# One level of Strassen's scheme in the up-projection of an MLP: seven half-width products instead of eight, with GpSimd forming the weight sums

## The chip, the cores and the metric

The kernel runs on one core of a Trainium2 chip. The time is device microseconds of one launch, the median of several executions. The engines are TensorE (PE in the profile, its weight loads PEld), VectorE (DVE), ScalarE (ACT), GpSimd (POOL) and SyncE (SP, which here issues the weight loads).

## The reference, cut to what matters

Two layers act on 512 tokens of width 1024, in float32. Each layer has three attention branches, whose gated sum goes through `w_out`, and then the MLP:

```python
x = x + merged @ w_out[l]
u = rmsnorm(x, g_mlp[l]) @ w_mlp1[l]                 # (512 x 1024) @ (1024 x 4096)
x = x + jnp.square(jax.nn.relu(u)) @ w_mlp2[l]       # (512 x 4096) @ (4096 x 1024)
```

## The kernel before, in words

Activations lie transposed: a tile is 128 features by 512 tokens. Every float32 matrix product is made of three passes in a rounded float32 format: an operand is split into a high part `hi` and a rest `lo`, and `mm3` adds hi x hi, hi x lo and lo x hi into one PSUM bank. A weight unit is 128 x 1024 floats (512 KB). It is loaded by SP into a raw buffer `wraw`, then ACT copies it, rounded, to `whi`, and DVE subtracts `whi` from `wraw` into `wlo`; this pair of instructions is called a split below. There are `RB` = 3 raw buffers and `NB` = 4 pairs of `whi` and `wlo`.

The program is a list of entries, each with the weight units it consumes. The loop at the end goes through it; ahead of each entry it emits splits up to `NB` units in front and loads up to `RB` units in front of those. A scheduler then orders the instructions of each engine and gives out buffers from free pools; within an engine instructions run strictly in the order that it wrote.

The end of a layer, which the change touches, is this sequence:

- eight `out_item`s: output projection, residual sum into the tile `X`, and `feed`, which makes the hi and lo tiles `h2` of the MLP's input (in pool `O`) and adds the squares up in `sq2`; after the last one `row_stats` turns the squares into the factors 1/rms of the tokens: PE sums over the features (`tok_sums`, line 236), DVE makes `ms`, POOL raises it to the power -1/2 (`r`), PE broadcasts `r` to all partitions (line 247), ACT copies this to `R`;
- `u_item`s, 32 a layer: 24 matmuls of 512 columns, DVE applies ReLU and `R2`, ACT squares twice, DVE makes the rest;
- `w2_item`s, 32 a layer: 24 matmuls of 512 columns on the up-projection's result, DVE adds them to `X`. They come in four stretches of eight, d(0) to d(3), one for each quarter `qr` of the 4096 features, in the order u0 u1 d0 u2 d1 u3 d2 d3.

In `chunk256`, which the change leaves alone, attention's projections use matmuls of 256 columns.

Of the kernel before, what the change touches and what calls it, by code (L numbers as in the profile page):

```python
# [9 lines left out]
F32 = mybir.dt.float32  # L10
# [49 lines left out]
def tile_trunk(ctx: ExitStack, tc: tile.TileContext, x_t, mem_t, mem_n, pos, ifr, gcol, grow, w_ck, w_cq, w_kvb, w_qb,  # L60
# [47 lines left out]
    def mm3(o, l, r, first, last):  # L108
        T.matmul(o, lhsT=l[0], rhs=r[0], start=first, stop=False)  # L109
        T.matmul(o, lhsT=l[0], rhs=r[1], start=False, stop=False)  # L110
        T.matmul(o, lhsT=l[1], rhs=r[0], start=False, stop=last)  # L111
# [28 lines left out]
    def trig():  # L140
# [44 lines left out]
        G.dma_start(out=lvt.rearrange("p (l d) -> p l d", l=L), in_=grow[:, 128:384].partition_broadcast(P))  # L185
# [93 lines left out]
    def layer(l):  # L279
# [13 lines left out]
        def begin():  # L293
            if l == 0:
# [464 lines left out]
        def y8_item(ft):  # L759
            def fn(w):  # L760
# [4 lines left out]
                hi, lo = tl("H", F32R), tl("H", F32R)  # L765
# [7 lines left out]
        def out_item(ft):  # L773
            def fn(w):
# [9 lines left out]
                if ft == KT - 1:  # L784
                    _, _, s["R2"] = row_stats(s["sq2"])
            return Entry(fn, [w_out[l, ft]])

        def u_item(qr, j):
            def fn(w):
                q = ps("s")  # L790
                for k in range(KT):
                    mm3(q, (w[0][0][:, k, :], w[0][1][:, k, :]), s["h2"][k], k == 0, k == KT - 1)
                z = tl("scr")
                V.scalar_tensor_tensor(out=z, in0=q, scalar=0.0, in1=s["R2"], op0=ALU.max, op1=ALU.mult)
                hi, lo = (tl("H" if qr % 2 == 0 else "B", F32R) for _ in range(2))
                A.activation(out=hi, in_=z, func=AF.Square)
                A.activation(out=z, in_=z, func=AF.Square)
                V.tensor_tensor(out=lo, in0=z, in1=hi, op=ALU.subtract)
                s.setdefault(("u", qr), []).append((hi, lo))
            return Entry(fn, [w_1[l, qr * 8 + j]])  # L800

        def w2_item(qr, ft):
            def fn(w):
                q = ps("acc")
                for k in range(KT):
                    mm3(q, (w[0][0][:, k, :], w[0][1][:, k, :]), s["u", qr][k], k == 0, k == KT - 1)
# [9 lines left out]
                st["h"].append(feed(l + 1, ft, xt, C_MIX, "H", st["sqs"]))  # L816
# [48 lines left out]
    units = [ap for e in prog for ap in e.units]  # L865
    raws, splits = [], []
    consumed = 0

    def load_raw():
        ap = units[len(raws)]  # L870
        a, b = ap.shape[1], ap.shape[2]
        t = pw_raw.tile([P, 1024], F32, tag="wraw", name=nm("wraw"))
        nc.sync.dma_start(out=t[:, :a * b].rearrange("p (a b) -> p a b", a=a), in_=ap)
        raws.append((t, a, b))
# [102 lines left out]
```

## Time and profile before

| what | us |
|---|---|
| median of 3 runs | 2050.37 (2050.34 to 2050.54) |
| span of the profiled execution, first to last instruction | 2047.5 |
| what lies around the span, by the median | 2.9 |
| PE busy | 2025.8 |
| DVE busy | 1125.5 |
| ACT busy | 870.5 |
| POOL busy | 152.4 |

The profiled execution's own time is not given beside its span; its span and the median differ by 2.9 us, and the sums are made with that. The profile is a page and the answers that the trace of the same execution gives: groups of instructions by line, engine and shape, with busy time and the mean of one; waits by who waited for whom; timelines; and stretches with each engine's busy time. The time at a row's start in a timeline is in us from the span's start. A busy PE counts overlapping matmuls once, so its busy time is not matmul work; the distance from start to start is.

### The profile page before, as it was taken

The numbers are of one execution on the slowest core, as the hardware profiler recorded it, in microseconds if no ns is written. First come the engines' busy times: TensorE is split into PE (matmuls) and PEld (weight loads), VectorE is DVE, ScalarE is ACT, GpSimd is POOL, SyncE is SP. The second block draws the span as 40 slices with busy tenths as digits, with TensorE's granted clock in tenths as the row PEclk, the third lists the DMA queues.
The fourth block names the chain that finished last, engine by engine and source line by source line (L and its number), as shares of the span: only waits on it lengthen the run. The fifth ranks groups of instructions, "written<-read, shape, count | busy, mean of one in ns | idle before, by whom it ended". The sixth has DMA issues, their size and how long they took to land.

```text
span 2047.5 us, 28283 instructions
## 1 busy us (share of the span) xinstructions
PE 2025.8 (99%) x11280; PEld 1735.7 (85%) x11280; DVE 1125.5 (55%) x2058; ACT 870.5 (43%) x1607; POOL 152.4 (7%) x125
## 2 busy tenths in 40 slices
PE   8999999999999999999999999999999999999999
PEld 7889997888878888888888999978897788888887
DVE  7754665667656443443457546657685554434442
ACT  6565543444443442322345645444454334323221
POOL 2300110101100000000003001101020000000000
PEclk9999999999999999999999999999999999999999
DMA  5242122222214333333333321212222233333332
GB/s 178 78 140 74 63 65 60 73 73 63 73 48 150 96 97 94 102 93 101 118 95 94 115 72 63 67 58 73 73 63 63 92 124 93 94 102 93 101 94 73
DMA packets 54036, 181.09 MB, mean 88 GB/s; under 512 B 6176, under 2 KB 6704, under 8 KB 53904
## 3 DMA queue, kind: packets, MB, share of 16 engines
q1 hardware_dynamic: 51840, 175.66, 28.0%
q10 hardware_dynamic: 1872, 3.21, 0.5%
q8 instruction: 89, 1.46, 0.3%
q0 software_dynamic: 192, 0.41, 0.1%
q14 instruction: 43, 0.35, 0.1%
HBM read 175.06 MB, written 4.19 MB: 88 GB/s over the span
## 4 chain that ended last, share of the span: by engine, by line
PE 97%; ACT 1%; DMA 1%; DVE 1%; issue 0%; SPq 0%; POOL 0%; POOLq 0%; ACTq 0%
PE psacc L109 21%; PE psacc L110 20%; PE psacc L111 20%; PE pss L109 7%; PE pss L110 7%; PE pss L111 7%; PE pso L642 4%; PE pss L609 3%; PE pss L612 2%; PE pstp L638 2%; PE pstp L649 1%; PE pstp L590 1%; PE pstp L478 1%; DMA X<-in_x_t_dram 0%; DMA B<-in_mem_n_dram 0%; PE pstp L236 0%
## 5 line engine op out<-in xcount | busy, mean ns | idle before, releaser
L101 ACT ACTIVATE whi<-wraw 128x1024 fp32r<-128x1024 f32 (+3 forms) x320 | 334.5, 1047 | 726.8 <-PE psacc L110 354.5
L102 DVE TENSOR_TENSOR wlo<-wraw,whi 128x1024 fp32r<-128x1024 f32 (+3 forms) x320 | 386.0, 1207 | 103.1 <-ACT whi L101 101.8
L109 PE MATMUL psacc<-H,whi 128*128 128x512 f32 x816 | 322.0, 395 | 1.3 <-ACT B L560 1.3
L110 PE MATMUL psacc<-H,whi 128*128 128x512 f32 x816 | 321.1, 393 | 0.0
L111 PE MATMUL psacc<-H,wlo 128*128 128x512 f32 x816 | 319.6, 392 | 0.0
L109 PE MATMUL psacc<-whi,H 128*128 128x256 f32 (+1 forms) x928 | 272.8, 295 | 7.2 <-ACT whi L101 5.8
L110 PE MATMUL psacc<-wlo,H 128*128 128x256 f32 (+1 forms) x928 | 265.9, 287 | 0.5 <-DVE wlo L102 0.5
L111 PE MATMUL psacc<-whi,H 128*128 128x256 f32 (+1 forms) x928 | 265.4, 287 | 0.0
L109 PE MATMUL pss<-O,whi 128*128 128x512 f32 x640 | 249.4, 391 | 1.6 <-ACT O L105 1.6
L110 PE MATMUL pss<-O,whi 128*128 128x512 f32 x640 | 249.7, 390 | 0.0
L111 PE MATMUL pss<-O,wlo 128*128 128x512 f32 x640 | 249.4, 390 | 0.0
L109 PEld LDWEIGHTS psacc<-whi,H 128*128 128x128 f32 x928 | 176.9, 191 | 15.6 <-ACT whi L101 6.0
L109 PEld LDWEIGHTS psacc<-H,whi 128*128 128x128 f32 x816 | 153.3, 188 | 34.7 <-ACT B L560 1.7
L110 PEld LDWEIGHTS psacc<-H,whi 128*128 128x128 f32 x816 | 153.3, 188 | 32.4 <-issue 1.5
L111 PEld LDWEIGHTS psacc<-H,wlo 128*128 128x128 f32 x816 | 153.3, 188 | 32.4 <-issue 1.5
L110 PEld LDWEIGHTS psacc<-wlo,H 128*128 128x128 f32 x928 | 177.6, 191 | 3.2 <-issue 1.4
L111 PEld LDWEIGHTS psacc<-whi,H 128*128 128x128 f32 x928 | 177.0, 191 | 0.0
L808 DVE TENSOR_TENSOR X<-psacc,X 128x512 f32<-128x512 f32 x64 | 44.3, 692 | 207.1 <-PE psacc L111 207.1
L109 PEld LDWEIGHTS pss<-O,whi 128*128 128x128 f32 x640 | 120.0, 188 | 28.3 <-ACT O L105 2.0
L110 PEld LDWEIGHTS pss<-O,whi 128*128 128x128 f32 x640 | 120.2, 188 | 25.2 <-DVE O L106 0.5
L111 PEld LDWEIGHTS pss<-O,wlo 128*128 128x128 f32 x640 | 120.2, 188 | 24.5
L626 ACT ACTIVATE P<-pss,nmx 128x128 f32<-128x128 f32 (+2 forms) x224 | 115.2, 521 | 51.3 <-DVE nmx L623 44.0
(223 smaller groups left out, 3139.6 us busy)
## 6 DMA issues: line engine op xcount, KB each, us to landing
wraw<-in_w_dram SPq DMA_DIRECT2D x128, 512.0 KB, 3.6
wraw<-in_w_g_dram SPq DMA_DIRECT2D x48, 512.0 KB, 3.6
wraw<-in_w_d_dram SPq DMA_DIRECT2D x48, 512.0 KB, 3.8
wraw<-in_w_mem_dram SPq DMA_DIRECT2D x16, 512.0 KB, 3.9
wraw<-in_w_od_dram SPq DMA_DIRECT2D x16, 512.0 KB, 3.5
wraw<-in_w_out_dram SPq DMA_DIRECT2D x16, 512.0 KB, 3.8
X<-in_x_t_dram SPq DMA_DIRECT2D x16, 256.0 KB, 6.3
wraw<-in_w_xq_dram SPq DMA_DIRECT2D x8, 512.0 KB, 3.8
```

The lines of the kernel that those rows point to most:

```text
L101: A.activation(out=hi, in_=src, func=AF.Copy)
L102: V.tensor_tensor(out=lo, in0=src, in1=hi, op=ALU.subtract)
L109: T.matmul(o, lhsT=l[0], rhs=r[0], start=first, stop=False)
L110: T.matmul(o, lhsT=l[0], rhs=r[1], start=False, stop=False)
L111: T.matmul(o, lhsT=l[1], rhs=r[0], start=False, stop=last)
L478: T.transpose(tp_[:96, t * P:(t + 1) * P], in_=src[t][:, h * 96:(h + 1) * 96], identity=ident)
L609: T.matmul(sw[m][:, :max(N, 256)], lhsT=qk[m][0][a], rhs=qk[m][1][b], start=i == 0, stop=i == 2)
L612: T.matmul(sv[m], lhsT=qk[m][0], rhs=qk[m][1], start=True, stop=True)
L626: A.activation(out=pt[:, m, :N], in_=sv[m], func=AF.Exp, bias=nmx[:, m:m + 1], accum_out=ssum[m])
L638: T.transpose(tp_[:, n * P:(n + 1) * P], in_=pt[:, m, j * P:(j + 1) * P], identity=ident)
L642: T.matmul(o_out[m], lhsT=w[:, n * P:(n + 1) * P], rhs=vs[m](j), start=j == 0, stop=j == nb - 1)
L808: V.tensor_tensor(out=xt, in0=q, in1=xt, op=ALU.add)
```

## The change

The up-projection of a layer is a product of a 1024 x 4096 matrix and the 1024 x 512 activations. The change cuts the tokens into two halves of 256, the 1024 input features into two of 512, and, in each of eight groups of 512 output features, these into two of 256. Strassen's scheme in its form with fifteen additions then makes the four blocks of a group from seven products in place of eight.

Token side: `a11` is the first half of the features for the first half of the tokens, `a21` the same for the second half, `a12` and `a22` the second half of the features. `mlp_sums` makes s1 = a21 + a22, s2 = s1 - a11, s3 = a11 - a21 and s4 = a12 - s2 once a layer, in the last four output items, and splits them. Weight side, for each group: t1 = b12 - b11, t2 = b22 - t1, t3 = b22 - b12 and t4 = b21 - t2, on GpSimd, in raw buffers (t3 in place of b12). A group's products, in PE's order, with the PSUM bank that they add into:

| product | operands | bank | what is done when it ends |
|---|---|---|---|
| 11 | a11, b11 | X | ACT copies X to p1 |
| 3 | s3, t3 | Y | |
| 2 | s2, t2 | X, added | ACT copies X to u2; DVE: u3 = Y + u2 |
| 1 | s1, t1 | Z | DVE: half of c1 = Z + u3 |
| 22 | a22, t4 | Y, added | DVE: half of c0 = Y + u2 |
| 4 | s4, b22 | Z, added | DVE: other half of c1 = Z + u2; `finish(1)` |
| 12 | a12, b21 | W | DVE: other half of c0 = W + p1; `finish(0)` |

Each product is 24 matmuls of 256 columns: 2 blocks of 128 output features x 4 input tiles x 3 passes. `finish` applies ReLU and `R2` to a tile of 128 x 1024, squares and splits it.

The pieces of weight are split in the order b11, t3, t2, t1, t4, b22, b21, with three pairs of `whi`/`wlo` in place of four and seven raw buffers in place of three. The pool `H` goes; its tiles come from `B`, now of 40; `scr` has 6. `row_stats` of the MLP becomes an entry of its own behind the second product. The order of the stretches is g0 g1 g2 d0 g3 g4 d1 g5 g6 d2 g7 d3. Four small DMAs at the start move from POOL's queue to ACT's.

```diff
-    RB, NB = 3, 4
+    RAW, NB = 7, 3
-    pools = {... (("H", 16), ("O", 16), ("X", 8), ("G", 1), ("B", 22), ("scr", 5), ("PT", 2))}
+    pools = {... (("O", 16), ("X", 8), ("G", 1), ("B", 40), ("scr", 6), ("PT", 2))}
...
-    G.dma_start(out=posi, in_=pos)
+    A.dma_start(out=posi, in_=pos)
...
     (out_item)
-                if ft == KT - 1:
-                    _, _, s["R2"] = row_stats(s["sq2"])
+                if ft >= 4:
+                    mlp_sums(ft - 4)
...
+        def mlp_sums(k):
+            ha, hb_ = tl("scr"), tl("scr")
+            scale_to(ha, s["x"][k], col(C_MLP + k))
+            scale_to(hb_, s["x"][k + 4], col(C_MLP + k + 4))
+            a11, a21, a12, a22 = ha[:, :256], ha[:, 256:], hb_[:, :256], hb_[:, 256:]
+            ta, tb = tl("scr"), tl("scr")
+            s1, s2, s3, s4 = ta[:, :256], ta[:, 256:], tb[:, :256], tb[:, 256:]
+            V.tensor_tensor(out=s3, in0=a11, in1=a21, op=ALU.subtract)
+            V.tensor_tensor(out=s1, in0=a21, in1=a22, op=ALU.add)
+            V.tensor_tensor(out=s2, in0=s1, in1=a11, op=ALU.subtract)
+            V.tensor_tensor(out=s4, in0=a12, in1=s2, op=ALU.subtract)
...
-        def u_item(qr, j):
...
+        def u_group(g):
...
+                    for sub in range(2):
+                        for k in range(4):
+                            mm3(q[:, sub * 256:(sub + 1) * 256], (w[0][0][:, k, sub * P:(sub + 1) * P], ...), side(i, k), ...)
...
+                    elif i == "2":
+                        z["u2"] = tl("scr")
+                        A.activation(out=z["u2"], in_=q, func=AF.Copy)
+                        z["u3"] = tl("scr")
+                        V.tensor_tensor(out=z["u3"], in0=z["Y"], in1=z["u2"], op=ALU.add)
...
+            def finish(j):
+                c = z["c%d" % j]
+                V.scalar_tensor_tensor(out=c, in0=c, scalar=0.0, in1=s["R2"]..., op0=ALU.max, op1=ALU.mult)
+                hl = [(tl("B", F32R), tl("B", F32R)) for _ in range(2)]
+                for i in range(2):
+                    A.activation(out=hl[i][0], in_=c[:, i, :], func=AF.Square)
+                A.activation(out=c, in_=c, func=AF.Square)
+                for i in range(2):
+                    V.tensor_tensor(out=hl[i][1], in0=c[:, i, :], in1=hl[i][0], op=ALU.subtract)
...
-        e += u(0) + u(1) + d(0) + u(2) + d(1) + u(3) + d(2) + d(3)
+        u0 = u_group(0)
+        e += u0[:2] + [Entry(mlp_stats)] + u0[2:] + u_group(1) + u_group(2)
+        e += d(0) + u_group(3) + u_group(4) + d(1) + u_group(5) + u_group(6) + d(2) + u_group(7) + d(3)
...
+            steps += [("load", b12), ("load", b11), ("sub", t1, b12, b11), ("load", b22), ("sub", t2, b22, t1), ("into", t3, b22, b12),
+                      ("load", b21), ("sub", t4, b21, t2)]
+            pieces += [b11, t3, t2, t1, t4, b22, b21]
...
+    def prep_step():
...
+            G.tensor_tensor(out=d["t"], in0=src[0]["t"], in1=src[1]["t"], op=ALU.subtract)
```

Where the rows stand. On DVE in the middle of the up-projection, before: `wlo` is a split, line 794 the ReLU of an item and line 798 its rest. One split, one ReLU and one rest go with each item of 24 full-width matmuls.

```order
L794 SCALAR_TENSOR_TENSOR scr_7273<-pss_7248,R_7010 128x512
L102 TENSOR_TENSOR wlo_7281<-wraw_7170,whi_7280 128x1024
L798 TENSOR_TENSOR H_7276<-scr_7273,H_7275 128x512
L794 SCALAR_TENSOR_TENSOR scr_7311<-pss_7286,R_7010 128x512
L102 TENSOR_TENSOR wlo_7319<-wraw_7208,whi_7318 128x1024
```

On DVE in the changed kernel, from the split of t1 of group 3 (`wlo_8117`) on: t4, b22, then line 836, which makes u3, 839 the first half of c1, the split of b21, 842 the first half of c0, the split of the next group's b11, 844 and 853 the end and the ReLU of c1.

```order
L103 TENSOR_TENSOR wlo_8117<-wraw_7862,whi_8116 128x1024
L103 TENSOR_TENSOR wlo_8148<-wraw_7991,whi_8147 128x1024
L103 TENSOR_TENSOR wlo_8183<-wraw_7894,whi_8182 128x1024
L836 TENSOR_TENSOR scr_8180<-pss_8122,scr_8178 128x512
L839 TENSOR_TENSOR c_8213<-pss_8188,scr_8180 128x2x256
L103 TENSOR_TENSOR wlo_8216<-wraw_7959,whi_8215 128x1024
L842 TENSOR_TENSOR c_8245<-pss_8122,scr_8178 128x2x256
L103 TENSOR_TENSOR wlo_8248<-wraw_8055,whi_8247 128x1024
L844 TENSOR_TENSOR c_8213<-pss_8188,scr_8178 128x2x256
L853 SCALAR_TENSOR_TENSOR c_8213<-c_8213,R_7153 128x1024
```

A split now stands between most of the instructions that empty a bank, and u3 is behind the split of the group's sixth piece, b22. It is the same in all sixteen groups, and on ACT too, where line 831 makes p1 and line 834 makes u2:

```order
L102 ACTIVATE whi_8116<-wraw_7862 128x1024
L831 ACTIVATE scr_8114<-pss_8089 128x512
L102 ACTIVATE whi_8147<-wraw_7991 128x1024
L102 ACTIVATE whi_8182<-wraw_7894 128x1024
L834 ACTIVATE scr_8178<-pss_8089 128x512
```

Here u2 is behind the rounding of b22 (`whi_8182`). On PE, the first two matmuls of product 1 stand ahead of product 2, and the other 22 behind it.

At the entry to the up-projection of layer 0, DVE before, from the residual sum of the last output item (line 782) on: a split, the rest of `feed`, the sum of squares, a split, then `ms`, from which POOL makes `r`.

```order
L782 SCALAR_TENSOR_TENSOR X_6683<-psacc_6963,X_6683 128x512
L102 TENSOR_TENSOR wlo_7015<-wraw_6883,whi_7014 128x1024
L106 SCALAR_TENSOR_TENSOR O_6990<-X_6683,gc,O_6989 128x512
L227 TENSOR_TENSOR scr_6691<-scr_6691,scr_6993 128x512
L102 TENSOR_TENSOR wlo_7053<-wraw_6922,whi_7052 128x1024
L242 TENSOR_SCALAR ms_7001<-pstp_6996 128x4
```

The same place on DVE in the changed kernel, from that residual sum (line 783) to `ms`; lines 796, 797 and 799 are s3, s1 and s4 of `mlp_sums`:

```order
L783 SCALAR_TENSOR_TENSOR X_6682<-psacc_7017,X_6682 128x512
L799 TENSOR_TENSOR scr_6998<-scr_6994,scr_6997 128x256
L103 TENSOR_TENSOR wlo_7069<-wraw_6804,whi_7068 128x1024
L103 TENSOR_TENSOR B_7004<-scr_6997,B_7003 128x512
L107 SCALAR_TENSOR_TENSOR O_7044<-X_6682,gc,O_7043 128x512
L228 TENSOR_TENSOR scr_6690<-scr_6690,scr_7047 128x512
L796 TENSOR_TENSOR scr_7055<-scr_7050 128x256
L103 TENSOR_TENSOR B_7008<-scr_6998,B_7007 128x512
L797 TENSOR_TENSOR scr_7054<-scr_7050,scr_7051 128x256
L103 TENSOR_TENSOR wlo_7102<-wraw_6726,whi_7101 128x1024
L243 TENSOR_SCALAR ms_7144<-pstp_7139 128x4
```

Five instructions more stand ahead of `ms`. On POOL, `r` follows the first subtraction for group 1:

```order
L973 TENSOR_TENSOR wraw_6901<-wraw_6844,wraw_6804 128x1024
L973 TENSOR_TENSOR wraw_7072<-wraw_6958,wraw_7015 128x1024
L133 TENSOR_TENSOR r_7146<-ms_7144,mhalf 128x4
L973 TENSOR_TENSOR wraw_6958<-wraw_7105,wraw_6958 128x1024
L973 TENSOR_TENSOR wraw_7136<-wraw_7105,wraw_7072 128x1024
```

Before, POOL had only `r` there.

More of the change, by code (lines that the diff above doesn't have):

```diff
@@ L863, in tile_trunk @@
         prog.extend(layer(l))
[L865 to L874, printed above, removed]
+    steps, pieces = [], []
+    for e in prog:
+        if e.group:
+            b11, b12, b21, b22 = ({"ap": ap} for ap in e.group)
+            t1, t2, t4 = {}, {}, {}
+            t3 = b12
+            steps += [("load", b12), ("load", b11), ("sub", t1, b12, b11), ("load", b22), ("sub", t2, b22, t1), ("into", t3, b22, b12),
+                      ("load", b21), ("sub", t4, b21, t2)]
+            pieces += [b11, t3, t2, t1, t4, b22, b21]
+        for ap in e.units:
+            d = {"ap": ap}
+            steps.append(("load", d))
+            pieces.append(d)
@@ new lines, in tile_trunk, with ready, wraw @@
+    last = {}
+    for n, (kind, d, *src) in enumerate(steps):
+        for x in (d, *src):
+            last[id(x)] = n
+    at, made, consumed, live = [0], [], 0, [0]
+    def ready(d):
+        return last[id(d)] < at[0]
+    def wraw(d, a, b):
+        d["t"], d["ab"] = pw_raw.tile([P, 1024], F32, tag="wraw", name=nm("wraw")), (a, b)
+        live[0] += 1
+    def prep_step():
+        kind, d, *src = steps[at[0]]
+        at[0] += 1
+        if kind == "load":
+            a, b = d["ap"].shape[1], d["ap"].shape[2]
+            wraw(d, a, b)
+            nc.sync.dma_start(out=d["t"][:, :a * b].rearrange("p (a b) -> p a b", a=a), in_=d["ap"])
+        else:
+            if kind == "sub":
+                wraw(d, *src[0]["ab"])
+            G.tensor_tensor(out=d["t"], in0=src[0]["t"], in1=src[1]["t"], op=ALU.subtract)
@@ L883, in tile_trunk @@
+        live[0] -= 1
     for i, e in enumerate(prog):
@@ L886, in tile_trunk @@
             continue
-        while len(splits) < min(len(units), consumed + NB):
-            while len(raws) < min(len(units), len(splits) + RB):
-                load_raw()
+        while True:
+            while at[0] < len(steps) and live[0] + (steps[at[0]][0] != "into") <= RAW:
+                prep_step()
+            if len(made) >= min(len(pieces), consumed + NB) or not ready(pieces[len(made)]):
+                break
             do_split()
-        while len(raws) < min(len(units), len(splits) + RB):
-            load_raw()
-        n = len(e.units)
-        e.fn(splits[consumed:consumed + n])
+        n = e.take
+        assert consumed + n <= len(made)
+        e.fn(made[consumed:consumed + n])
         consumed += n
```

107 lines of the change are left out of this document (73 added, 34 removed).

## The prediction

> **What bounds the kernel now.** I read the page's shares, clock and chain first, then what the matrix engine waits for, then the stretches that are touched.
>
> ```profile
> PE 2025.8 (99%) x11280; PEld 1735.7 (85%) x11280; DVE 1125.5 (55%) x2058; ACT 870.5 (43%) x1607; POOL 152.4 (7%) x125
> PEclk9999999999999999999999999999999999999999
> PE 97%; ACT 1%; DMA 1%; DVE 1%; issue 0%; SPq 0%; POOL 0%; POOLq 0%; ACTq 0%
> PE psacc L109 <- ACT whi L101: 5.8, 2, 5.6
> PE pstp L649 <- DVE scr L646: 2.8, 4, 0.8
> 633.88:677.40 43.52, 43.52 (x194) 36.04 (x192) 24.70 (x31) 17.06 (x23) 0.00 (x0) 1.00 0.36 111
> 766.38:809.90 43.52, 43.52 (x194) 36.05 (x192) 15.98 (x17) 9.65 (x11) 0.00 (x0) 1.00 0.33 97
> 677.40 0.39 PE L109 MATMUL pss<-O,whi 128*128 128x512 f32 x1
> 766.38 0.39 PE L109 MATMUL psacc<-H,whi 128*128 128x512 f32 x1
> 809.90 0.39 PE L109 MATMUL pss<-O,whi 128*128 128x512 f32 x1
> ```
>
> PE works 99% of the span and is 97% of the chain, at the full clock; it waits 5.6 us at the start and under a microsecond elsewhere. So only matmul time can be saved, and every new wait of PE is paid in full. The two window rows are the eight output-projection items and one w2 stretch of layer 0: 192 matmuls take 43.52 us, **0.2267 us each**, while DVE is busy 24.7 and 16.0 us. The up-projection's first sixteen items run from 677.40 to 766.38, 88.98 us; 16 x 5.44 is 87.04. The entry costs 1.94 us there.
>
> **What the change takes away.** Per layer 32 items of 24 full-width matmuls, 768 x 0.2267 = 174.1 us, become 8 groups of 7 products of 24 half-width matmuls, 1344. Their price is read where half-width ones follow each other undisturbed:
>
> ```profile
> 506.25 0.39 PE L109 MATMUL psacc<-whi,H 128*128 128x256 f32 x1 [0.70 <-ACT scr L563]
> 506.47 0.28 PE L110 MATMUL psacc<-wlo,H 128*128 128x256 f32 x1
> 513.90 0.28 PE L109 MATMUL psacc<-whi,H 128*128 128x256 f32 x1
> ```
>
> 62 spacings in 7.43 us are **0.1198 us**; after a wait the first spacing is 0.22. So 1344 x 0.1198 = 161.0 us: **13.1 us saved per layer**, and a product lasts 2.88 us, a group 20.1.
>
> **What it adds, per group.** Durations of the kinds of instruction added:
>
> ```profile
> L102 DVE TENSOR_TENSOR wlo<-wraw,whi 128x1024 fp32r<-128x1024 f32 x306 | 374.0, 1223 | 100.1 <-ACT whi L101 99.1 <-PE pstp L420 0.7
> L101 ACT ACTIVATE whi<-wraw 128x1024 fp32r<-128x1024 f32 x306 | 324.0, 1060 | 707.0 <-PE psacc L110 344.5 <-PE pss L110 213.5 <-issue 72.2
> L794 DVE SCALAR_TENSOR_TENSOR scr<-pss,R 128x512 f32<-128x512 f32 x64 | 43.9, 691 | 160.5 <-PE pss L111 154.0 <-ACT R L249 6.5
> L797 ACT ACTIVATE scr<-scr 128x512 f32<-128x512 f32 x64 | 40.5, 633 | 2.0
> L582 DVE TENSOR_TENSOR scr<-scr,rb 128x256 f32<-128x256 f32 x64 | 24.2, 420 | 0.0
> L106 DVE SCALAR_TENSOR_TENSOR O<-X,gc,O 128x512 fp32r<-128x512 f32 x16 | 11.9, 746 | 0.0
> 739.15 1.06 ACT L101 ACTIVATE whi<-wraw 128x1024 fp32r<-128x1024 f32 x1 [3.19 <-PE pss L110]
> 739.18 0.39 PE L109 MATMUL pss<-O,whi 128*128 128x512 f32 x1
> 739.38 0.69 DVE L794 SCALAR_TENSOR_TENSOR scr<-pss,R 128x512 f32<-128x512 f32 x1 [2.69 <-PE pss L111]
> 740.25 1.23 DVE L102 TENSOR_TENSOR wlo<-wraw,whi 128x1024 fp32r<-128x1024 f32 x1 [0.18 <-ACT whi L101]
> 741.43 0.69 DVE L798 TENSOR_TENSOR B<-scr,B 128x512 fp32r<-128x512 f32 x1
> wraw<-in_w_dram SPq DMA_DIRECT2D x128, 512.0 KB, 3.6
> ```
>
> DVE: seven splits (1.18 from start to start, 740.25 to 741.43), nine half-tile additions and differences (0.64), two full-width ReLUs (1.18): 8.3 + 5.8 + 2.4 = 16.4 us of 20.1. ACT: seven splits, two copies, four squares of 0.63, two of 1.06: 13.3 us. Neither is the bound by itself. The loads stay 512 KB each, four a group.
>
> *Wait at product 22.* Product 22 adds onto bank Y, from which u3 must have been read. u3 stands on DVE behind the split of the sixth piece, and u2, which it needs, on ACT behind that split's first half. That split needs the weight buffer that product 2 frees, three buffers back. Counting from the first matmul behind product 2: the ACT half starts at 0.1 (739.15 beside 739.18, shorter matmuls), ends at 1.16; u2 ends at 1.8; the DVE half runs from 1.19, u3 from 2.37 to 3.06. PE meanwhile has the other 22 matmuls of product 1, 2.64 us. It waits 0.45 us and restarts 0.1 slower: **0.55 us** in each group. Ends 0 (a split ready early) and 0.7.
>
> *GpSimd's subtractions.* Four of 128x1024 a group, two SBUF inputs each, like most of DVE's work. The trace shows how the two meet:
>
> ```profile
> 489.95 0.95 DVE L584 TENSOR_TENSOR scr<-scr,scr 128x512 f32<-128x512 f32 x1
> 489.82 0.53 POOL L290 TENSOR_TENSOR rb<-sind,gr 128x128 f32<-128x128 f32 x1
> L584 DVE TENSOR_TENSOR scr<-scr,scr 128x512 f32<-128x512 f32 x32 | 21.6, 691 | 0.1
> 511.33 5.67 POOL L132 TENSOR_TENSOR f<-e,mhalf 128x8 f32<-128x8 f32 x1
> L132 POOL TENSOR_TENSOR r<-ms,mhalf 128x4 f32<-128x4 f32 x4 | 4.1, 1018 | 544.0 <-ACT O L408 352.9 <-DVE ms L242 191.1
> 48.76 1.72 POOL L289 TENSOR_TENSOR ra<-cosd,gr 128x128 f32<-128x128 f32 x4
> ```
>
> A DVE sum that met a POOL product of 128 elements took 0.95 instead of 0.69: held 0.26. A POOL power of eight elements that met a run of DVE sums took 5.67 us. So either holds the other. [...] Eight times the length gives a hold of **2.06 us** per subtraction; ends 0 and 3.4 (8 x 1.72/4, the whole instruction). [...]
>
> Where do they fall? Seven raw buffers let group g+1 be prepared while g runs, but not behind a w2 stretch's units: the subtractions fall beside groups 0, 1, 3 and 5, the others' in light stretches. The subtraction for t3 waits for the load of b22, which waits for the buffer freed by the fourth piece's split: 2.88 + 0.1 + 1.06 + 0.03 + 1.22 = 5.3 us into the group, + 3.6 = 8.9, held to 10.95. The split ahead of u3 is ready at 8.87 + 1.19 = 10.06: 0.9 us late, so **1.45 us** in groups 1, 3 and 5 (ends 0.55 and 2.85), 0.55 in 2, 4, 6, 7.
>
> *Entry to the up-projection.* Each of the last four output items gets four half-width differences and two splits more on DVE, 5.6 us of work per 5.44 us item, so DVE arrives full. From the end of the last item the DVE rows ahead of ms sum to 7.2 us, 6.6 with their overlap; ms at 6.8. [...] In PE's order the broadcast of r stands behind 53 matmuls and the token sums, at 7.8 us. PE waits 2.2 us there and 0.6 for the token sums, which before were nearly hidden: **2.5 us** over the old 1.94, and group 0 then has its 1.45. Ends 0.5 (r first) and 6 (starved to the run's end, hold 3.4).
>
> *The rest.* A split buffer less starts each split an item later; two items of 5.44 us, or two products, 5.76, still cover its 2.3: nothing in the stretches above, and where short attention items leave only one, between 0 and 2.3; I take 0.5, near the low end, since PE waits nowhere for a split before except at the start. The last group before the last w2 stretch is covered by the twelve plus twelve matmuls on the older groups, 5.4 us. The moved small DMAs: nothing, ACT waits for loads then.
>
> **Sum, per layer:** 13.1 - (4 x 0.55) - (3 x 1.45) - (2.5 + 1.45) - 0.5 = 2.1 us, two layers 4.2. Span 2047.5 + 2.9 around it is the median 2050.4; the forecast is **2046.2**. All low costs: 13.1 - 0.5 = 12.6 a layer, 2025; all high: 13.1 - 2.8 - 8.6 - 8.9 - 2.3 = -9.5, 2069.
>
> **Rivals.** *Faster: POOL is out of the way.* If its reads fall into DVE's gaps (16.4 of 20.1 us leaves 3.7, and five of DVE's additions read a bank), all eight groups cost 0.55 and the entry 0.5: 13.1 - 5.4 = 7.7 a layer, **2035**. For it: the one long DVE hold shown is 0.26. Against: 8.2 us of holds against 3.7 idle.
>
> *Slower: DVE becomes the bound beside POOL.* 16.4 + 8.2 = 24.6 us in groups 0, 1, 3 and 5 against PE's 20.1: 4.5 us each if every hold delays the queue, 2.75 if the holds fall evenly on busy and idle time (16.4 + 6.5 against 20.7, + 0.55). With the quiet groups, entry and splits (5.2) that is 23.2 or 16.2 a layer against 13.1: 2070.6 or 2056.6, middle **2063**. It decides from 2.0 us per such group on. Against it: the last differences of a group may lag into the next without PE noticing.
>
> *The halves cost more than half.* Zero gain is at 174.1 / 1344 = 0.1295. With one 0.2 us restart per product the spacing is 0.123 and the gain 8.8: **2055**. The undisturbed run speaks against it.
>
> **Chances.** Forecast 0.33, POOL out of the way 0.34, DVE bound 0.27, dear halves 0.06. The forecast's own range, 2040 to 2052, straddles the edge of what can be told from no change (0.2%, 4.1 us): about half of it counts as faster. Faster 0.49, same 0.24, slower 0.27. The range for eight in ten is 2033 to 2065.
>
> **What the next profile would show.** Half-width matmuls 0.12 apart; PE waiting before product 22 for DVE's u3, about 0.5 us, longer in groups 1, 3 and 5 than in 2, 4, 6, 7; splits longer than 1.22 us wherever a POOL subtraction runs; a wait for r of some 2 us at the entry. Wrong would be: no waits before 22, splits at 1.22 beside POOL, or POOL's subtractions stretched in place of DVE's work, so that weights come late and PE waits for ACT's first half.

## The result: slower, 2069.0 us for 2050.4

The changed kernel takes 2069.03 us (median of 4, 2065.54 to 2078.07), before 2050.45: 1.0097 times as long, 95% interval 1.0072 to 1.0122. The profiled execution is the one of 2065.54 us, with a span of 2063.8, 16.3 us above that of before. Ratios here and below leave out disturbed executions; medians don't.

The page, its busy times and its chain:

```profile
PE 2014.7 (98%) x12432; PEld 1778.5 (86%) x12432; DVE 1297.2 (63%) x2202; ACT 943.3 (46%) x1687; POOL 311.4 (15%) x185
PEclk9999999999999999999999999999999999999999
PE 63%; DVE 4%; ACT 2%; issue 1%; DMA 0%; POOL 0%; DVEq 0%; POOLq 0%; ACTq 0%
```

PE is still busy 98% of the span, 11 us less than before, in a span that is 16 us longer. Two things happen, and these rows hide the second: PE waits, and while it is busy it is at times slow. The clock's row reads 9 throughout, as before, since a slice is 52 us long and anything above 0.9 is a 9. First the waits (what PE waited for, us in total, times, the longest):

```profile
PE pss L110 <- DVE scr L836: 11.8, 14, 1.9
PE psacc L110 <- ACT whi L102: 7.0, 1, 7.0
PE pstp L237 <- DVE scr L228: 5.5, 2, 2.7
PE pso L643 <- ACT PT L96: 3.0, 4, 1.4
PE pss L110 <- ACT B L102: 2.7, 2, 1.3
```

Line 836 is u3, the wait before product 22. Line 237 is the token sums at the entry, waiting for the sum of squares. The first matmul of the program starts at 7.0 us in place of 5.6, and `PT` is a wait in the attention. Then the clock, by stretches (span, PE, PEld, DVE, ACT and POOL busy with counts, granted clock, DMA share, GB/s). The first two rows are the MLPs of both layers, the others single stretches of 3.41 or 6.83 us:

```profile
681.84:1036.87 355.03, 343.28 (x2129) 310.87 (x2128) 228.68 (x239) 146.18 (x176) 73.23 (x29) 0.99 0.32 105
1704.59:2060.00 355.41, 345.05 (x2129) 312.62 (x2127) 216.64 (x224) 136.40 (x160) 72.35 (x29) 0.98 0.28 93
689.97:696.80 6.83, 6.75 (x32) 6.79 (x33) 4.49 (x10) 1.75 (x3) 2.30 (x2) 0.50 0.24 79
809.44:812.85 3.41, 1.92 (x16) 1.71 (x15) 3.12 (x2) 1.80 (x3) 3.41 (x2) 1.00 0.00 0
812.85:816.26 3.41, 3.01 (x25) 3.02 (x26) 2.96 (x3) 0.00 (x0) 2.03 (x2) 1.00 0.46 159
1830.02:1833.43 3.41, 1.50 (x14) 1.30 (x12) 3.31 (x2) 1.34 (x2) 3.41 (x2) 1.00 0.00 0
1833.43:1836.85 3.42, 3.42 (x16) 3.42 (x17) 2.60 (x2) 0.00 (x0) 2.20 (x2) 0.50 0.46 158
1836.85:1840.26 3.41, 3.41 (x31) 3.41 (x30) 1.92 (x2) 1.06 (x1) 1.71 (x1) 1.00 0.00 0
```

From 1833.43 on, 3.4 us run at clock 0.50: 16 half-width matmuls start where the next 3.4 us have 31, and PE counts as fully busy in both. It stands right behind a wait of 1.91 us for u3. All changes of the clock in this execution lie whole multiples of 3.413 us apart; a stretch between two neighbouring points of this grid is called a cell below. The same wait in layer 0, 1.89 us, spread over two cells (809.44 to 812.85 and on), left the clock full. In the profiled execution the clock is halved from 126.77 for 3.41 us, from 689.97 and 1710.55 for 6.83 each (the entries), from 1833.43 and 1922.18 for 3.41 each: 23.9 us, a loss of up to 11.9.

By stages, from the starts of the matmuls:

| stage | before | after | difference |
|---|---|---|---|
| to the first output item of layer 0 | 633.88 | 638.32 | +4.4 |
| MLP, layer 0 | 350.12 | 355.03 | +4.9 |
| attention, layer 1 | 622.37 | 624.20 | +1.8 |
| MLP, layer 1 | 350.11 | 355.41 | +5.3 |

The output items take 43.52 us in all four cases. The four rows sum to 16.4, the spans differ by 16.3.

### The profile page after: what moved, and what is told of

Read it like the earlier page. It is cut to its first block, busy times and chain, and to the rows that moved or that the text cites. A ratio compares the mean times of both kernels' runs of the same rounds, so it can differ in the third digit from the quotient of the medians.

```text
span 2063.8 us, 30987 instructions
## 1 busy us (share of the span) xinstructions
PE 2014.7 (98%) x12432; PEld 1778.5 (86%) x12432; DVE 1297.2 (63%) x2202; ACT 943.3 (46%) x1687; POOL 311.4 (15%) x185
## 4 chain that ended last, share of the span: by engine, by line
PE 63%; DVE 4%; ACT 2%; issue 1%; DMA 0%; POOL 0%; DVEq 0%; POOLq 0%; ACTq 0%
PE psacc L110 13%; PE psacc L111 13%; PE psacc L112 13%; PE pss L110 5%; PE pss L111 5%; PE pss L112 5%; PE pso L643 2%; DVE wlo L103 2%; PE pss L610 2%; PE pss L613 1%; PE pstp L639 1%; ACT whi L102 1%; PE pstp L111 1%; PE pstp L110 1%; PE pstp L112 1%
## 5 line engine op out<-in xcount | busy, mean ns | idle before, releaser
L110 PE MATMUL psacc<-B,whi 128*128 128x512 f32 x1072 | 420.4, 392 | 1.3 <-ACT B L561 1.3
L111 PE MATMUL psacc<-B,whi 128*128 128x512 f32 x1072 | 420.8, 393 | 0.0
L112 PE MATMUL psacc<-B,wlo 128*128 128x512 f32 x1072 | 419.5, 391 | 0.0
L110 PE MATMUL psacc<-whi,B 128*128 128x256 f32 (+3 forms) x1008 | 301.6, 300 | 9.2 <-ACT whi L102 7.0
L111 PE MATMUL psacc<-wlo,B 128*128 128x256 f32 (+3 forms) x1008 | 295.4, 294 | 0.0
L112 PE MATMUL psacc<-whi,B 128*128 128x256 f32 (+3 forms) x1008 | 293.6, 293 | 0.6 <-DVE B L107 0.6
L973 POOL TENSOR_TENSOR wraw<-wraw,wraw 128x1024 f32<-128x1024 f32 x64 | 165.6, 2595 | 537.6 <-DVE wlo L103 366.9
L110 PEld LDWEIGHTS psacc<-B,whi 128*128 128x128 f32 x1072 | 201.3, 188 | 44.2 <-ACT B L561 2.2
L112 PEld LDWEIGHTS psacc<-B,wlo 128*128 128x128 f32 x1072 | 201.4, 188 | 42.6 <-issue 1.5
L111 PEld LDWEIGHTS psacc<-B,whi 128*128 128x128 f32 x1072 | 201.3, 188 | 42.4 <-issue 1.5
L110 PEld LDWEIGHTS psacc<-whi,B 128*128 128x128 f32 x1008 | 192.1, 191 | 19.8 <-ACT whi L102 7.0
L111 PEld LDWEIGHTS psacc<-wlo,B 128*128 128x128 f32 x1008 | 192.5, 191 | 3.4 <-issue 1.0
L112 PEld LDWEIGHTS psacc<-whi,B 128*128 128x128 f32 x1008 | 191.9, 191 | 2.1 <-DVE B L107 0.8
L110 PE MATMUL pss<-B,whi 128*128 128x256 f32 x512 | 146.2, 287 | 2.7 <-ACT B L102 2.7
L111 PE MATMUL pss<-B,whi 128*128 128x256 f32 x512 | 145.3, 286 | 0.0
L110 PE MATMUL pss<-O,whi 128*128 128x256 f32 (+1 forms) x384 | 126.0, 330 | 14.3 <-DVE scr L836 11.8
```

The lines of the kernel that those rows point to most:

```text
L110: T.matmul(o, lhsT=l[0], rhs=r[0], start=first, stop=False, **kw)
L111: T.matmul(o, lhsT=l[0], rhs=r[1], start=False, stop=False, **kw)
L112: T.matmul(o, lhsT=l[1], rhs=r[0], start=False, stop=last, **kw)
L973: G.tensor_tensor(out=d["t"], in0=src[0]["t"], in1=src[1]["t"], op=ALU.subtract)
```

## The experiments

One table for all; "half clock" is what the profiled execution has of it in us, without start and end.

| run | edit | median us | against before (95%) | span | half clock |
|---|---|---|---|---|---|
| layout | before, with the new buffers only | 2059.71 | 1.0036 (1.0022 to 1.0050) | 2057.4 | 13.7 |
| dma_sp | layout, ACT's loads on SP | 2050.53 | 0.9998 (0.9989 to 1.0008) | 2048.5 | 0 |
| loads_sp | the change, ACT's loads on SP | 2063.49 | 1.0051 (1.0033 to 1.0069) | 2062.5 | 30.7 |
| no_sums | the change, sums left out | 2045.54 | 0.9973 (0.9961 to 0.9985) | 2041.1 | 10.2 |
| sums_dve | the change, sums on DVE | 2054.13 | 1.0012 (0.9996 to 1.0028) | 2053.4 | 23.9 |
| u3_first | the change, u3 before a split | 2055.00 | 1.0019 (1.0008 to 1.0031) | 2052.0 | 27.3 |
| tok_late | the change, token sums later | 2067.20 | 1.0076 (1.0050 to 1.0101) | 2066.9 | 37.5 |
| spread | the change, items reordered | 2063.10 | 1.0061 (1.0037 to 1.0084) | 2057.7 | 23.9 |
| gaps | before, with waits put in | 2306.61 | one execution | 2304.8 | 174 |
| best | loads_sp + u3_first + spread | 2037.98 | 0.9932 (0.9915 to 0.9949) | 2036.1 | 6.8 |
| best_r_first | best, r before the sums | 2037.65 | 0.9938 (0.9924 to 0.9951) | 2038.4 | 17.1 |
| best_late4 | best, token sums later | 2038.68 | 0.9939 (0.9927 to 0.9951) | 2035.6 | 6.8 |
| best_dve | best, sums on DVE | 2029.10 | 0.9895 (0.9880 to 0.9909) | 2026.4 | 0 |
| best_no_sums | best, sums left out | 2025.11 | 0.9876 (0.9863 to 0.9888) | 2021.7 | 0 |

### The buffers alone, and the queue that loads stand in

```diff
-    RB, NB = 3, 4                 (before)
+    RB, NB = 7, 3                 (layout; pools and small loads as in the change)
-            A.dma_start(out=mt, ...)            (layout)
+            nc.sync.dma_start(out=mt, ...)      (dma_sp, loads_sp; likewise posi, fr, gr, mem_t, the lambdas)
```

> The kernel before with the changed kernel's buffers alone: seven raw buffers, three pairs of hi and lo, the pool H in B (40), six scr, the four small DMAs on ACT's queue; the arithmetic and the up-projection are those of before. In the changed kernel the start and the attention of layer 0 end 4.4 us later than before (638.32 against 633.88) and layer 1's 1.8 us longer. Theory: the buffers alone do that, so about 2056 us, with the first matmul at 7.0 us. Rival: it comes from the new MLP next door (its loads and subtractions run ahead into the attention), and this kernel stays at 2050. The prediction had 0.5 us a layer.

Measured 2059.7: the buffers alone cost more than the whole prediction gave them. First matmul at 7.0 us; and, on ACT and PE at 124 us (start, length, engine, line, tiles, and in brackets the wait):

```profile
123.67 0.63 ACT L206 ACTIVATE B<-B 128x512 f32<-128x512 f32 x1 [3.02 <-DMA B<-in_mem_n_dram]
124.30 0.36 ACT L95 ACTIVATE PT<-pstp 128x256 f32<-128x256 f32 x1
124.72 0.66 PE L642 MATMUL pso<-B,PT 128*128 128x64 f32 x4 [1.59 <-ACT PT L95]
125.75:139.40 13.65, 13.18 (x48) 10.78 (x49) 5.20 (x14) 9.40 (x29) 0.70 (x1) 0.50 0.42 136
```

ACT stands 3.02 us in front of a square whose operand a load is still bringing; the copy `PT` that PE needs is queued behind it. PE waits 1.59 us, then 0.85 for the next piece from ACT, and then come 13.65 us at half clock (the last row, a stretch). Before, the same square waited for its load too, and the copy came right behind it, but 3.3 us sooner:

```profile
120.37 0.63 ACT L206 ACTIVATE B<-B 128x512 f32<-128x512 f32 x1 [2.86 <-DMA B<-in_mem_n_dram]
121.42 0.66 PE L642 MATMUL pso<-B,PT 128*128 128x64 f32 x4 [0.25 <-ACT PT L95]
```

PE still had a projection to do then and waited 0.25 us. At the start, ACT's `ACT_TABLE_LOAD` (1.28 us) runs at 1.18 before, while the first tile of x is on its way, and at 3.84 in layout, when the tile is there.

> The kernel of the run on the buffers alone (layout), with the loads that ACT issues, all but the first (gc), moved to SP's queue: three small ones behind the tiles of x, and the loads of mem and of the lambdas. The layout's own changed places were the first matmul (7.0 us in place of 5.6), and a PE wait of 1.59 + 0.85 us at 125 us for a copy that stood on ACT behind a square that waits for a load which ACT had issued late, with 13.65 us at half clock behind it. Theory (the queue order on ACT, made by the moved loads and new buffers, is the layout's cost): first matmul at 5.6, no wait above 1 us at 125, full clock, about 2050. Rival (three pairs of hi and lo in place of four starve short attention items): 2056 to 2060 stays.

The theory held for the time: 2050.5, no change from before, with three pairs and the new pools kept.

```profile
PE psacc L109 <- ACT whi L101: 5.6, 1, 5.6
PE pso L643 <- ACT PT L95: 2.3, 4, 1.4
```

So with the arithmetic of before the missing pair of `whi` and `wlo` costs nothing; the cost was the loads in ACT's queue, and `ACT_TABLE_LOAD` runs at 1.17 again. At 123.0 a wait of 1.35 us is left, longer than the theory allowed, without slow clock behind it. The run also moves the loads of mem, which stood on ACT before the change too, so it doesn't tell their part from that of the four moved loads.

> The changed kernel with the loads that ACT issues, all but gc, on SP's queue, and nothing else. Theory (the start and the attention of layer 0 cost 4.4 us through ACT's queue, as dma_sp against layout shows for the buffers alone): first matmul at 5.6 us, no slow clock at 126 us, output items of layer 0 from 634 instead of 638.3; the MLP as before: 2059 to 2062 in undisturbed executions. Rival (the waits elsewhere take it back): 2065 or more.

In the changed kernel the same edit gave 2063.5, between the theory and the rival, and less than expected in its profile: the start is mended (first matmul at 5.75, no slow clock at 126), but another stretch takes its place. The same 3.4 us and the 10.24 behind them, in loads_sp and then in before:

```profile
344.20:347.60 3.40, 2.02 (x12) 1.46 (x12) 2.93 (x6) 1.75 (x6) 0.00 (x0) 1.00 0.12 46
347.60:357.84 10.24, 10.24 (x28) 7.24 (x28) 5.78 (x18) 3.68 (x13) 0.00 (x0) 0.50 0.01 2
344.20:347.60 3.40, 2.02 (x13) 1.33 (x13) 2.52 (x6) 1.51 (x4) 0.00 (x0) 1.00 0.37 135
347.60:357.84 10.24, 10.24 (x54) 7.47 (x54) 9.02 (x25) 5.70 (x16) 0.00 (x0) 1.00 0.01 2
```

Both wait 1.38 us there, in narrow attention products; one loses the clock for 10.24 us (28 matmuls for 54), the other does not. This risk is in the kernel before too, and not of the change: one of its later executions, of 2057.7 us, has a mean clock of 0.995.

### GpSimd's subtractions

```diff
-            G.tensor_tensor(out=d["t"], in0=src[0]["t"], in1=src[1]["t"], op=ALU.subtract)
+            d["t"] = src[0]["t"]                                                              (no_sums)
+            V.tensor_tensor(out=d["t"], in0=src[0]["t"], in1=src[1]["t"], op=ALU.subtract)    (sums_dve)
```

> The changed kernel without GpSimd's 64 subtractions: t1, t2 and t4 are read from the raw buffers of b12, b22 and b21, so the weight sums are left out and all else is kept. Theory (GpSimd's reads hold DVE's splits): splits of 1.22 us everywhere, the wait before product 22 at 0.25 to 0.5 us in all groups in place of 1.2 to 1.9 in groups 0, 1, 3 and 5, the wait for the token sums under 1 us, the clock full: the 12 us of longer waits, 4 of the entry and 10 of half clock go, about 2041 us. Rival 1 (DVE's own work is too much at the entry): the 2.7 us wait and its slow clock stay, about 2052. Rival 2 (GpSimd does not matter): 2065.

2045.5, near the theory's 2041 (the clock was not full: the profiled execution, 2042.9, has 10.24 us at half clock in the attention). The wait before product 22 is 0.25 us in all fourteen groups that have one, for 11.8 in all in the changed kernel:

```profile
PE pss L110 <- DVE scr L836: 3.5, 14, 0.3
```

In the changed kernel, the page's groups of splits and of subtractions (count, busy, mean ns, idle before):

```profile
L103 DVE TENSOR_TENSOR wlo<-wraw,whi 128x1024 fp32r<-128x1024 f32 (+3 forms) x368 | 475.4, 1293 | 139.5 <-ACT whi L102 138.7
L973 POOL TENSOR_TENSOR wraw<-wraw,wraw 128x1024 f32<-128x1024 f32 x64 | 165.6, 2595 | 537.6 <-DVE wlo L103 366.9
```

A subtraction takes 2.6 us on average. What it does to DVE, in group 3 of layer 0:

```profile
809.11 5.72 POOL L973 TENSOR_TENSOR wraw<-wraw,wraw 128x1024 f32<-128x1024 f32 x2 [4.54 <-DMA wraw<-in_w_dram]
809.73 2.86 DVE L103 TENSOR_TENSOR wlo<-wraw,whi 128x1024 fp32r<-128x1024 f32 x1 [1.84 <-ACT whi L102]
812.51 0.68 DVE L836 TENSOR_TENSOR scr<-pss,scr 128x512 f32<-128x512 f32 x1
813.25 0.39 PE L110 MATMUL pss<-O,whi 128*128 128x256 f32 x1 [1.89 <-DVE scr L836]
```

The split ahead of u3 takes 2.86 us in place of 1.22, u3 follows, PE waits 1.89.

> The changed kernel with the weight sums on DVE in place of GpSimd and nothing else. Theory (the engine chosen for the sums is the larger part of the miss, by holding DVE's splits): splits of 1.22 us, the wait before product 22 at 0.25 to 0.55 us in all groups, no slow clock behind it; 4.9 us more of DVE's own work a group are partly seen at the entry, where DVE is full: 2046 to 2052, against 2045.5 without any sums. Rival (the order in the queues is the miss, and sums on DVE are 4.9 us more in that order): the waits stay, 2060 to 2068.

2054.1, the same time as the kernel before within the interval, between theory and rival and nearer the theory. The engine by itself was worth 15 us, and the order of the queues still costs; the waits for u3 are fewer, but reach 1.2 us, and in layer 1 the clock halves behind a cell with one of them and 1.03 us for a rounding. The first two waits of PE are now

```profile
PE pstp L110 <- ACT whi L102: 6.2, 6, 1.0
PE pss L110 <- DVE scr L836: 4.0, 10, 1.2
```

### u3 ahead of the sixth split

```diff
-        split_into(hi[:, :n], lo[:, :n], t[:, :n])
+        with issue_after(u2), issue_after(u3):      # for the piece b22 alone
+            split_into(hi[:, :n], lo[:, :n], t[:, :n])
```

> The changed kernel with the split of the sixth piece (b22) issued behind u2 on ACT and behind u3 on DVE. Theory (u3 is late because it stands behind that split): the 11.8 us of waits before product 22 go, and the two stretches of 3.4 us at half clock behind two of them (3.4 us): about 2051 in a profiled execution. Rival (DVE is late as a whole beside GpSimd, the place in the queue does not matter): the waits turn up before product 4 or 12, about 2061 to 2065.

The theory held for the wait: of the 11.8 us for u3 one wait of 0.92 is left, in the first group, though GpSimd's subtractions and their holds are all still there. So a hold cost PE here where the instruction behind it was one that PE waits for. The median is 2055.0, the profiled execution 2053.8 for the 2051 expected; it had 10.24 us of half clock at 127 and 10.24 and 6.83 at the entries.

### The entry to the up-projection

DVE, POOL and PE at the entry of layer 0 in the changed kernel:

```profile
685.85 0.68 DVE L103 TENSOR_TENSOR B<-scr,B 128x512 fp32r<-128x512 f32 x1
686.07 2.68 POOL L973 TENSOR_TENSOR wraw<-wraw,wraw 128x1024 f32<-128x1024 f32 x1 [15.29 <-DVE wlo L103]
686.46 2.84 DVE L107 SCALAR_TENSOR_TENSOR O<-X,gc,O 128x512 fp32r<-128x512 f32 x1
689.22 0.68 DVE L228 TENSOR_TENSOR scr<-scr,scr 128x512 f32<-128x512 f32 x1
690.04 1.84 PE L237 MATMUL pstp<-ones,scr 128*128 128x1 f32 x8 [2.73 <-DVE scr L228]
```

The subtraction for group 1 starts as soon as its buffer is free, in the middle of DVE's run, and holds the last item's rest for 2.1 us; the sum of squares and PE follow it.

```diff
+            x = T.matmul(q[:, t:t + 1], lhsT=sqs[...], rhs=ones, ...); keep_in_program_order(x)    (tok_late)
-        e += [out_item(ft) for ft in range(KT)]
+        e += [out_item(ft) for ft in (0, 4, 1, 5, 2, 6, 3, 7)]                                     (spread)
```

> The changed kernel with the token sums on PE held behind all 48 matmuls of the first two products of group 0, where the program has them, instead of behind seven. Theory (a wait costs its own length and then the half clock that follows it): PE has 5.4 us of work while DVE finishes the squares, the 2.73 us wait goes, and the 6.8 us at half clock behind it too, 3.2 us: together about 6 us a layer, 2053 to 2057 against 2065.5 in the profiled executions, and the slow clock there gone. Rival 1 (the slow clock has nothing to do with the wait): the wait goes and the slow clock stays, 2060. Rival 2 (the wait moves on, to r or to the end of group 0): 2064 to 2067.

Rival 2: 2067.2. The wait of 1.34 stays, and in place of the 2.73 there are 1.18 us for the rounding of a weight on ACT and 1.60 for the low part of the sums of tokens on DVE; 6.83 us at half clock stay in both layers. PE had more to do and still came to the end of it before DVE.

> The changed kernel with the eight output items in the order 0 4 1 5 2 6 3 7, so that the sums of tokens (s1 to s4) fall due after every second item instead of after each of the last four. Theory (DVE is full when it gets to the entry, 5.6 us of work for each of the last four items of 5.44 us and GpSimd's holds on top): only the last pair is left at the end, the waits at the entry fall from 1.34 + 2.73 + 1.43 us to under 1.5 together and the 6.8 us at half clock go: about 7 us a layer, 2051 to 2055 in a profiled execution. Rival (the last item alone and GpSimd's subtraction beside it make the wait): 1.5 us a layer or nothing, 2062 to 2066.

2063.1; the entry's waits fell from 4.07 to 1.69 us in layer 0 and 2.03 in layer 1, the 1.43 of layer 0 is gone, but 6.83 us at half clock stayed in both. The theory was half right: the waits fell, though not under 1.5 us, but the clock halved behind cells with only 1.04 us of waiting in layer 0 and 0.64 in layer 1.

### When the clock halves

```diff
+    def chain(q, n):                       # behind each up-projection item of before
+        a = small("chain", 1, 1)
+        V.tensor_copy(out=a, in_=q[:, 511:512])
+        for _ in range(n):
+            G.tensor_copy(out=a, in_=a)
+        keep_in_program_order(T.matmul(ps("tp")[:, :1], lhsT=ident, rhs=a, start=True, stop=True))
```

> The kernel before with a wait put into PE's stream behind each of the 64 up-projection items: DVE copies one column of the item's bank, GpSimd copies it in place n times (n = item number mod 10), and a one-column matmul on it, pinned in order, holds PE until then; the results are those of before. Waits of some 0.5 to several us, eight or so of each length. In the changed kernel waits of 1.74 and 1.91 us were followed by 3.41 us at half clock, 1.88 and 1.89 twice by none, and all changes of the clock stand on one grid of 3.413 us; counted by cells of that grid the first two have 1.74 and 1.91 us of waiting in one cell, the others 1.49 and 1.56. Theory: the clock halves at a cell's end when more than half of the cell (1.71 us) was waiting, and comes back after a busy one; so no wait under 1.5 us does it, one of 2 to 3 us does it in half to nearly all cases by its place on the grid, one over 3.4 always, and each costs 1.7 us or more beyond itself. Rival: only a cell idle as a whole does it, so waits under 3.4 us leave the clock full, and the changes of the changed kernel have another cause.

The waits came out up to 4.0 us, 133 us of them in all, and 174 us of the span ran at half clock. All changes of the clock stand on whole multiples of 3.413 us from the first one. Of the cells that began at full clock, every one with 2.07 us of waiting or more was followed by half clock (37), and none with 1.30 or less; no such cell lay between. The one nearest from below and from above, each with its following cell:

```profile
813.24:816.65 3.41, 2.12 (x10) 1.42 (x8) 1.15 (x3) 1.46 (x2) 0.79 (x4) 1.00 0.02 7
816.65:820.06 3.41, 2.48 (x12) 2.11 (x13) 1.52 (x2) 0.86 (x2) 0.88 (x1) 1.00 0.39 120
721.08:724.49 3.41, 1.19 (x7) 0.72 (x6) 2.64 (x4) 2.32 (x3) 1.66 (x4) 1.00 0.00 0
724.49:727.90 3.41, 3.41 (x10) 2.63 (x9) 0.04 (x1) 0.00 (x0) 0.00 (x0) 0.50 0.52 154
```

(The second pair is one of several with 2.22 us; the cell with 2.07 lies in the attention.) The groups of all the runs here, away from the entries, fill in between: full clock after up to 1.69 us of waiting in a cell (loads_sp, 897.1), half from 1.74 on (the changed kernel, 1918.8). The theory's 1.71 lies between the two. In this run the clock came back behind cells with at most 0.08 us of waiting and stayed at half behind those with 0.21 and more. The theory held in the stretches of dense matmuls, the rival did not. Not settled is what decides elsewhere: in cells near the token sums the clock fell after waits of 0.64 and 1.04 us too (spread), and at one entry it came back behind a cell with 0.48 (sums_dve, 1706.2). In the attention's narrow products it fell after 1.38 us in loads_sp, no_sums and best_r_first and not in before, best_dve and best_no_sums, and it stayed low through cells without any wait (loads_sp, 347.60 to 357.84).

### All three mended, and the sums moved

> Three edits of these runs together on the changed kernel: u3 ahead of the sixth split, the output items in the order 0 4 1 5 2 6 3 7, and the loads on SP's queue. If the three costs are separate (waits at product 22 with their clock about 15 us, the entry about 14, the start and the attention about 6): 2065.5 - 35 = 2030 to 2036. If the entry's wait comes from the last item, about 2045; if the layout's cost is the missing pair of buffers, 2040.

2038.0, 0.7% faster than before, and 2 us above the range for separate costs, in which the entry's cost goes as a whole. The first matmul starts at 5.64, no group waits for u3, and 2.03 us of waits and 3.41 us at half clock are left at each entry, about 3.7 us a layer.

```diff
+            for x in subtractions_of_group_1: add_manual_dep(x, r)             (best_r_first)
+        e += u0[:4] + [Entry(mlp_stats)] + u0[4:] + u_group(1) + u_group(2)    (best_late4, token sums pinned)
```

> The run with the three edits (best), and GpSimd's four subtractions for group 1 queued behind r. In best a half-width difference at the entry (s4, 683.57) took 2.49 us in place of 0.43 beside the first of them, PE waited 1.04 us for the token sums and 0.99 for the last pair's sums, and 3.41 us ran at half clock. Theory (this one hold is what is left of the entry): both waits and the slow clock go, 2.0 + 1.7 = about 3.5 us a layer, 2031. Rival 1 (DVE is late there anyway): one wait of 1 us stays, 2034 to 2036. Rival 2 (the subtractions, begun later, make group 1 wait for t3 or t2): 2038 or more.

Rival 1 by what is left, though the median, 2037.7, lies above its range: the second wait (0.99) goes, the first (1.04 for the token sums) stays with its slow clock. Group 0's own subtractions had held DVE during the output items: four of its instructions from 646.31 to 667.78 took 11.7 us in place of some 3.9, and DVE came to the end late. (The difference at 683.57 that the expectation calls s4 is s2.) Three executions took 2034.5 to 2035.2, three 2040.1 to 2043.8; the profiled one, of the second kind, has 10.24 us at half clock in layer 1's attention.

> The run best with the token sums held on PE behind the first four products of group 0. With the output items spread, 84 of these 96 matmuls need nothing of the last item but its own features, about 10 us, against DVE's 9.3 us to the last sums. Theory: PE has work while it waits, one wait under 0.6 us is left, the clock stays full, 2031 to 2034. Rival (as when the items were not spread, the wait only moves to the last pair's sums): 2036 to 2038.

The rival in time: the waits became 2.00, for the rounding of a weight that stands on ACT behind the last item's work, and 0.99, for the last pair's sums; no gain.

> The run best with the weight sums on DVE in place of GpSimd (1.22 us each, four a group). DVE then has 16.4 + 4.9 = 21.3 us of work in a group of 20.1, and 16 in a w2 stretch of 43. Theory (the sums belong off DVE, the holds fall into its gaps): entry and groups late, 4 to 10 us slower than best, 2042 to 2048. Rival (a GpSimd subtraction holds DVE as long as DVE would need, up to 2.2 us, and it shows): within 2 us of best or faster, 2034 to 2039.

The theory was wrong by its sign: 2029.1, 9 us faster than best and 1.05% (0.91 to 1.20) faster than before, the fastest kernel here that computes everything.

> The run best without GpSimd's subtractions (the weight sums are left out as in no_sums). It shows what their holds still cost after the order is mended. Theory (holds cost only where DVE's next instruction is one that PE waits for; with u3 ahead of the split that is the entry alone): 2 to 4 us a layer at the entry, 2030 to 2033. Rival 1 (they cost in every group): 2026 or less. Rival 2 (nothing): 2037.

2025.1, the time of rival 1, but at the theory's place: in layer 0 it is 7.1 us shorter than best from the first output item to the end of the MLP, of which the entry's waits and half clock make 3.7. Counted from the first output item, group 1 begins at 70.3 us in best and at 65.4 here, and the first w2 stretch at 112.4 and 105.8. So 4.9 of the 7.1 us arise before group 1, 1.8 in groups 1 and 2, and 0.5 in all the rest. The output items and the MLP of layer 0 together, in before, best, best_dve and best_no_sums (DVE's busy time is the third):

```profile
633.88:1027.52 393.64, 393.64 (x1746) 326.15 (x1745) 177.18 (x208) 131.36 (x169) 1.01 (x1) 1.00 0.34 102
634.04:1021.89 387.85, 385.23 (x2321) 345.32 (x2320) 268.33 (x280) 168.28 (x208) 85.55 (x33) 1.00 0.31 103
632.97:1016.38 383.41, 382.24 (x2322) 343.64 (x2321) 271.14 (x312) 169.87 (x208) 1.14 (x1) 1.00 0.32 105
633.57:1014.29 380.72, 380.72 (x2321) 343.21 (x2320) 236.90 (x280) 169.29 (x208) 1.12 (x1) 1.00 0.32 105
```

Without the sums the stretch is 12.9 us shorter than before, all of the saving. DVE is busy 236.9 us then, 271.1 when it makes the 32 sums itself, and 268.3 when GpSimd makes them: of 34 us of work given away 31 came back as held time, at places that DVE's queue could not choose. DVE has room for the sums (271 of 383 us); it has none for being stopped at the entry.

## Why the prediction was wrong

Forecast 2046.2, range 2033 to 2065, profiled execution 2065.5 and median 2069. Its steps:

- *The saving, 13.1 us a layer.* Right: 12.9 with the sums left out.
- *The full clock.* This is the step that failed by most. The profile of before shows clock 1.00 throughout, and the sum took it over with "every new wait of PE is paid in full": each wait was charged its own length and no more. Measured: 20.5 us at half clock in the two MLPs and 3.4 in the attention, up to 11.9 us, in the profiled execution; in the four executions, mean clocks of 0.994, 0.988, 0.990 and 0.994 with spans of 2063.8, 2076.3, 2070.6 and 2063.8. Take (1 - clock) x span off, and 2051.4, 2051.4, 2049.9 and 2051.4 are left. The clocks have three digits, so each of these is good to about 1 us. So the spread of the changed kernel is clock, and at full clock its span would have been about 4 us above before's 2047.5. In this execution 1.74 us of waiting in one cell of 3.413 us (1918.8) were followed by half clock in the next.
- *The entry, 2.5 us over the old 1.94.* The place was right, the path was not, and the size was too small. The 2.5 has 2.2 us for r in it, a term that no run shows: GpSimd's first subtraction got in at 686.07, in the middle of DVE's run, and held the last item's rest for 2.1 us. PE then waited 2.73 us for the token sums (0.6 predicted), 1.34 for the sums of tokens of the last pair but one (not predicted), and nothing for r; 1.43 more in layer 0 for a late split: 4.1 to 5.5 us, and 6.83 at half clock behind it.
- *"The moved small DMAs: nothing", and 0.5 for the missing pair.* Failed the other way round: the pair costs nothing (dma_sp, with the arithmetic of before), and the loads in ACT's queue cost the start 1.4 us and, with what was queued behind another load, the attention its wait and its slow clock. 4.4 us up to the first output item in the profiled execution; by the ratio of layout to before, 0.36%, 7 us in all.
- *The wait at product 22.* Right in place and cause: 0.55 in groups 2, 4, 6, 7, and 1.45 in 0, 1, 3, 5. Measured in layer 0: 0.25 to 0.26 in groups 2, 4, 6, 7; 1.18, 1.89 and 1.88 in groups 1, 3 and 5; 0.12 in group 0: some 6 us for 8.0 predicted. The hold, 2.06 estimated, is 1.64 and 2.09 us in the two rows shown (2.86 for 1.22, 2.84 for 0.75). At the entry the DVE instruction ended 0.55 us behind the subtraction (689.30 and 688.75), and alone it takes 0.75.
- *Rivals.* "DVE becomes the bound beside POOL", 2063, came nearest in time but not in kind: DVE is busy 229 us of 355 in the MLP, and mending one place in the order (u3_first) removes the groups' wait while DVE has as much to do. "POOL is out of the way", 2035 with a chance of 0.34, failed on the holds (splits that began beside a subtraction took up to 2.88 us in place of 1.22, while 25 of the additions that read a bank began beside one and took their 0.68 to 0.69), and is about what the kernel comes to when the order is mended (best, 2038).

In sum, in the profiled execution: -26 saving; +12 waits for u3; +9.6 waits at the entries; +4.5 start and attention (without their clock); up to +11.9 clock; the rest, some 4.5, was not put down to single places. The forecast had -26, +16, +5, +1 and nothing. So of the 20.5 us by which the profiled execution's span exceeds the forecast's, up to 11.9 are clock, 4.6 the entries, 3.5 the start and the attention, and 4.5 have no place; the waits for u3 were 4 less than forecast. That the sum with all costs high, 2069, is the median is luck: it has longer waits for u3 and nothing for the clock.

## What to carry to other kernels

The kernel here, at 99% PE and full clock, had a cliff beside it: a wait of 1.91 us was followed by 3.41 us at half clock (1833.43), up to 1.7 us more, and 1.38 us of waiting in narrow products by 10.24 us (loads_sp, 347.60), up to 5.1 more. So I would charge a change that adds waits of 1.7 to 3 us to such a kernel up to twice for them, an estimate from these rows. Holding PE's waiting matmuls back behind others only moved the waits here (tok_late, 2067.2 us for 2069.0; best_late4, 2038.7 for 2038.0); a better order on DVE and ACT, and sums that DVE makes itself, took most of them away. Before work goes to GpSimd to relieve DVE, count the time that DVE is held and where: here it gave away 34 us of sums a layer and was held for 31. A load issued from a computing engine's queue is a place in that queue (in layout ACT stood 3.02 us for one, and PE 1.59 for the copy behind it): look at what PE needs that stands behind the instruction that waits for it.

## What the hardware showed beyond that

- In stretches of dense matmuls the clock fell after a cell of 3.413 us with 1.74 us of waiting (the changed kernel, 1918.8) or more, 1.69 and less left it full (loads_sp, 897.1), and in gaps it rose only after a cell with at most 0.08. In the changed kernel a wait of 1.89 us, 1.49 of it in one cell and the rest in the next, left the clock full (809.44), and one of 1.91 us within a cell was followed by 3.41 us at half clock, up to 1.7 us more (1833.43).
- In the attention's narrow products the half clock often lasted longer: 10.24 us (loads_sp, no_sums, u3_first, best_r_first) or 13.65 us (layout, sums_dve, tok_late) behind cells with 1.4 to 2.3 us of waiting, and 3.41 us in the changed kernel.
- A run of DVE instructions did not keep GpSimd out: at the entry of the changed kernel the subtraction began (686.07) during a DVE instruction of 0.68 us (685.85), and it was the next one of DVE's that was held, 2.84 us in place of 0.75.
